# Where the down projection's operands begin: its weight chunks 160 bytes and the gated activations 96 bytes further on

## The chip, the core and the metric

The kernel runs on one core of one Trainium2 chip. The metric is the device time of one execution in microseconds; the kernel before took 497.76 us, the median of three runs between 497.63 and 497.88. Profiles are of one execution each. TensorE is written PE in the profile, its weight loads PEld, VectorE DVE, ScalarE ACT, GpSimd POOL, SyncE SP.

## What is computed

The program is one layer of a decoder trunk on 256 tokens of 1024 channels, in float32:

```python
mix = hybrid_mixer(x, w_in, ...)                 # mLSTM and attention branches, gated, projected
x = layer_norm(ALPHA * x + mix, ln1_g, ln1_b)
u = causal_dwconv(einsum("bsd,df->bsf", x, w_up), conv_ffn)      # 1024 -> 2 x 2816, 3 taps
g, up = split(u, 2)
ffn = einsum("bsf,fd->bsd", silu(g) * up, w_down)                # 2816 -> 1024
x = layer_norm(ALPHA * x + ffn, ln2_g, ln2_b)
```

The change is in the last three lines: `silu(g) * up` is what the text calls the gated activations, `w_down` the down projection.

## The kernel before

**Weights come as a stream of chunks.** `chunk_order` (line 45) lists 81 chunks of 128 x 2048 floats (1 MB) in the order of use: 4 "o", then four groups of 8 (qm, qb, km, kb, vm, vb, ga, gb), 8 for the branch projections (wa, wb), 4 for the output projection (wo), then the MLP: up 0 to 3, then eight times (dn d, up 2d+4, up 2d+5), then up 20, up 21, dn 8, dn 9, dn 10. The main loop of `run` (line 304) takes one chunk per turn. In a turn it issues the element work that the last step left, splits the chunk that is due in two steps, starts the DMA of the chunk five steps ahead on SyncE, and runs `step_<kind>`, which issues the matmuls.

**Every product is three products.** A float32 operand is kept as a high part in float32r (names ending in h) and a rest (l). `split_into` (line 92) makes them: a cast on ScalarE (line 94) and a subtraction on VectorE (line 95). `mm3` (line 125) then issues high x high, high x rest and rest x high, lines 128, 129 and 130, into the same accumulator. In `tensor.matmul(out, stationary, moving)` the second operand is loaded into the array by a LDWEIGHTS of 128 columns, and the third streams past it. So each line of `mm3` has one row of PE and one of PEld in the profile.

**Where an operand begins.** The high and rest parts of a chunk live in tiles of 2176 floats (8704 bytes, 34 x 256), three buffers each (tags "wh" and "wl"). `split_parts` (line 101) puts the chunk at an offset of `shift(kind, i)` floats in its tile:

```python
a = shift(*self.order[s])
wh, wl = wh[:, a:a + KT * 264], wl[:, a:a + KT * 264]
```

`shift` (line 61) is 48 for vm, vb, o; 56 for wa, wb; 8 for up 2; 0 for wo and dn; 16 for the rest. All slices that a matmul takes of an operand lie 512 or 1024 bytes apart (chunk 3 of "o" alone differs), so the start modulo 256 is the same for every matmul of a step. The program's allocation gives these starts (bytes modulo 256):

| step | moving operand | stationary operand | moving columns |
|---|---|---|---|
| o 0, o 1 | weights 64 | x 64 | 512 |
| qm, qb, km, kb, ga, gb | x 64 | weights 128 | 256 |
| vm, vb | weights 0 | x 64 (vm's first: a copy at 128) | 256 |
| wa, wb | y 224 | weights 32 | 256 |
| wo ("mix") | weights 64 | merged 128 | 256 |
| up 0, up 1 | weights 0 | x1 64 | 256 |
| up 2 | x1 64 | weights 96 | 256 |
| up 3 to 21 | x1 64 | weights 128 | 256 |
| dn, before | weights 64 | gated activations 128 | 512 and 256 |
| side work: pss, psl | 128 | 128 | 256 (and 128) |
| side work: pso | 224 | 128 | 256 (and 128) |

up 0 and up 1 have tiles of their own ("ahead").

**The MLP.** `step_up` (line 940) computes one chunk of the up projection, 48 matmuls of 256 moving columns into `ps_up`. `up_evac` (line 987) applies the three convolution taps (lines 999 and 1003, into `cu`), the gate, and splits the result into `hh` and `hl` (tags "hh" and "hlo", 128 x 256 float32r, six buffers each). These come from the pool "ffn", opened at `s == first["up"]` (line 328), and so do `tu`, `cu` and `nmr`. `step_dn` (line 1018) multiplies two such pairs (stationary) by one chunk of `w_down` (moving) into five accumulators called `ffn` that stay open for the whole MLP. For dn 0 to 7 that is 30 matmuls in the order: for each half of the chunk, 6 of 512 columns (tokens 0 to 127), then 3 of 512 and 6 of 256 (tokens 128 to 255). The last three chunks are taken together: 36 of 512 columns for the first tokens, 18 of 512 and then 36 of 256 for the others. In all there are 198 matmuls of 512 columns and 132 of 256. `finish` (line 1082) then normalises and stores the second half of the tokens.

Of the kernel before, what the change touches and what calls it, by code (L numbers as in the profile page):

```python
# [10 lines left out]
F32 = mybir.dt.float32  # L11
# [7 lines left out]
P = 128  # L19
# [41 lines left out]
def shift(kind, i):  # L61

    if (kind, i) == ("up", 2):

        return 8
    if kind in ("vm", "vb", "o"):
        return 48
    if kind in ("wa", "wb"):
        return 56
    return 0 if kind in ("wo", "dn") else 16  # L70


class Kernel:
# [27 lines left out]
    def split_parts(self, s):  # L101
        if s >= len(self.order) or s in self.w:
            return []
        raw = self.raw.pop(s)
        if s in self.extra:
            wh, wl = self.extra.pop(s)
        else:
            wh = self.stream.tile([P, WCOLS], F32R, tag="wh", name=f"wh{s}", bufs=3)
            wl = self.stream.tile([P, WCOLS], F32R, tag="wl", name=f"wl{s}", bufs=3)
            a = shift(*self.order[s])  # L110
            wh, wl = wh[:, a:a + KT * 264], wl[:, a:a + KT * 264]
        if s == 3:

            vh, vl = (t.rearrange("p (k f) -> p k f", k=KT) for t in (wh, wl))
            vr = raw.rearrange("p (k f) -> p k f", k=KT)
            cuts = [tuple(t[:, 4 * i:4 * i + 4, 0:256] for t in (vh, vl, vr)) for i in range(2)]
            cuts.append((vh[:, :, 256:264], vl[:, :, 256:264], self.wif))
        else:
            wh, wl = wh[:, 0:2048], wl[:, 0:2048]
            cuts = [tuple(t[:, i * 1024:(i + 1) * 1024] for t in (wh, wl, raw)) for i in range(2)]  # L120
        self.w[s] = (wh, wl)
        return [lambda c=c: self.split_into(*c) for c in cuts]
# [54 lines left out]
    def run(self):  # L177
# [126 lines left out]
        for s, (kind, i) in enumerate(self.order):  # L304
            if s == 8:
                self.elem_work(s, self.split_parts(s + 2))
                pre_cm.__exit__(None, None, None)
                self.open_att(att_cm.__enter__())
            if s == first["wa"]:
                self.elem_work(s)  # L310
                att_cm.__exit__(None, None, None)
                mix_cm.__exit__(None, None, None)
                self.open_post(post_cm.__enter__())
                mg = mg_cm.__enter__()
                self.mgh = mg.tile([P, KT, S], F32R, name="mgh")
                self.mgl = mg.tile([P, KT, S], F32R, name="mgl")
            if s == first["wo"]:
                self.elem_work(s)
                y_cm.__exit__(None, None, None)
                zp = ahead_cm.__enter__()  # L320
                for j in range(2):
                    self.extra[first["up"] + j] = tuple(
                        zp.tile([P, 2112], F32R, name=f"ahead{n}{j}")[:, 8:8 + 2048] for n in "hl")
            if s == first["up"]:
                self.elem_work(s)
                mg_cm.__exit__(None, None, None)
                self.fp = ffn_cm.__enter__()
            late = s == first["up"]
            self.elem_work(s, [] if late or s == 8 else self.split_parts(s + 2))
            self.load(s + 5)  # L330
            if s in (first["wo"], first["wo"] + 1):
                self.split(s + 4)
            getattr(self, "step_" + kind)(s, i, bo)
            for f in self.side_pe.pop(s, []):
                f()
            if late:
                self.split(s + 2)
# [832 lines left out]
```

## Time and profile before

| what | value |
|---|---|
| median of three runs | 497.76 us (497.63 to 497.88) |
| the profiled execution: its time | 497.07 us |
| its span, first to last instruction | 495.2 us |
| PE busy | 482.3 us, 3889 matmuls |
| DVE, ACT, POOL busy | 369.6, 288.4, 29.5 us |
| the MLP's matmuls, first to last | 298.2 to 486.1 us of the span |

A row of a group of instructions reads: line, engine, operation, output<-inputs, shape, count, busy time and mean duration of one, idle time of the engine just before. A matmul's duration holds its way through the array, so it is longer than the distance from its start to that of the next. This distance is called the **pitch** below. On an engine that never waits, the sum of the pitches is the time. A row of the timeline reads: start in us, duration in us, engine, line, operation, output<-inputs, shape, count.

### The profile page before, as it was taken

To read this page: it belongs to the slowest core of one execution; us is meant where nothing else is said; L and a number is where in the kernel's file an instruction comes from. 1 tells how busy PE (TensorE), PEld (TensorE's weight loads), DVE (VectorE), ACT (ScalarE), POOL (GpSimd) and SP (SyncE) were. 2 spreads that over 40 slices of the span, in tenths; PEclk is the share of its full clock that TensorE was granted. 3 is DMA by queue.
4 is the path that set the end of the run, shared out by engine and by line. 5 is a ranking of instruction groups with operands and counts; after the bars stand their busy time and mean duration, and the time that the engine had idled before them with its cause. 6 is when DMAs were issued, how large, how long until landed. Compare 5 with 4: busy or idle time off the path is not lost.

```text
span 495.2 us, 9470 instructions
## 1 busy us (share of the span) xinstructions
PE 482.3 (97%) x3889; PEld 466.5 (94%) x3889; DVE 369.6 (75%) x662; ACT 288.4 (58%) x478; POOL 29.5 (6%) x46
## 2 busy tenths in 40 slices
PE   7999999999999999999999999999999999999992
PEld 4899999999999999999999999999999999999982
DVE  5776995788588858885777788788667766866886
ACT  5657867495749665866655524666544555554610
POOL 0400011002000110002000001000000000000001
PEclk9999999999999999999999999999999999999997
DMA  7984555555554655444945672745555456444202
GB/s 254 359 300 151 204 191 205 177 179 184 193 173 175 196 180 187 169 171 148 364 171 182 222 276 86 255 148 205 212 203 177 164 185 241 171 171 171 86 1 85
DMA packets 19036, 93.74 MB, mean 189 GB/s; under 512 B 4625, under 2 KB 5913, under 8 KB 9009
## 3 DMA queue, kind: packets, MB, share of 16 engines
q1 hardware_dynamic: 14834, 87.08, 49.5%
q0 software_dynamic: 4160, 6.07, 3.9%
q8 instruction: 30, 0.49, 0.4%
q14 instruction: 12, 0.10, 0.1%
HBM read 92.05 MB, written 2.63 MB: 191 GB/s over the span
## 4 chain that ended last, share of the span: by engine, by line
PE 94%; DMA 2%; DVE 1%; SPq 1%; ACT 0%; issue 0%; POOL 0%; POOLq 0%
PE ps_up L130 8%; PE ps_up L128 8%; PE ps_up L129 8%; PE ffn L130 4%; PE ffn L129 4%; PE ffn L128 4%; PE ps_vm L128 2%; PE ps_qm L128 2%; PE ps_vm L130 2%; PE ps_vm L129 2%; PE ps_vb L130 1%; PE ps_vb L128 1%; PE ps_vb L129 1%; PE mix L128 1%; PE ps_wb L129 1%; PE ps_wa L129 1%
## 5 line engine op out<-in xcount | busy, mean ns | idle before, releaser
L95 DVE TENSOR_TENSOR wl<-raw,wh 128x1024 fp32r<-128x1024 f32 (+1 forms) x162 | 187.8, 1199 | 28.3 <-ACT wh L94 28.0
L94 ACT CAST wh<-raw 128x1024 fp32r<-128x1024 f32 (+1 forms) x162 | 158.8, 1030 | 10.8 <-DMA raw<-in_wst_dram 7.2
L128 PE MATMUL ps_up<-x1h,wh 128*128 128x256 f32 x320 | 90.0, 281 | 0.0
L130 PE MATMUL ps_up<-x1h,wl 128*128 128x256 f32 x320 | 89.9, 281 | 0.0
L129 PE MATMUL ps_up<-x1l,wh 128*128 128x256 f32 x320 | 89.9, 281 | 0.0
L129 PEld LDWEIGHTS ps_up<-x1l,wh 128*128 128x128 f32 x320 | 61.3, 192 | 0.0
L130 PEld LDWEIGHTS ps_up<-x1h,wl 128*128 128x128 f32 x320 | 60.1, 188 | 0.0
L128 PEld LDWEIGHTS ps_up<-x1h,wh 128*128 128x128 f32 x320 | 60.1, 188 | 0.0
L1003 DVE SCALAR_TENSOR_TENSOR cu<-ps_up,vec,cu 128x255 f32<-128x255 f32 (+1 forms) x80 | 33.0, 475 | 27.1 <-ACT cu L999 26.9
L130 PE MATMUL ffn<-wh,hl 128*128 128x512 f32 (+1 forms) x110 | 38.4, 349 | 0.0
L129 PE MATMUL ffn<-wl,hh 128*128 128x512 f32 (+1 forms) x110 | 38.4, 349 | 0.0
L128 PE MATMUL ffn<-wh,hh 128*128 128x512 f32 (+1 forms) x110 | 38.3, 349 | 0.0
L94 ACT CAST hh<-cu 128x256 fp32r<-128x256 f32 x22 | 8.9, 407 | 42.9 <-DVE cu L1011 42.9
L999 ACT ACTIVATE cu<-ps_up,vec 128x256 f32<-128x256 f32 x40 | 16.8, 471 | 28.8 <-PE ps_up L130 28.0
L129 PEld LDWEIGHTS ffn<-wl,hh 128*128 128x128 f32 x110 | 20.8, 189 | 3.0
L128 PEld LDWEIGHTS ffn<-wh,hh 128*128 128x128 f32 x110 | 20.7, 188 | 3.0
L130 PEld LDWEIGHTS ffn<-wh,hl 128*128 128x128 f32 x110 | 20.7, 188 | 2.9
L128 PE MATMUL ps_vb<-wh,xth 128*128 128x256 f32 x64 | 18.1, 283 | 0.0
L128 PE MATMUL ps_gb<-xth,wh 128*128 128x256 f32 x64 | 18.0, 282 | 0.0
L129 PE MATMUL ps_vm<-wl,xth 128*128 128x256 f32 x64 | 17.9, 280 | 0.0
L130 PE MATMUL ps_vm<-wh,xtl 128*128 128x256 f32 x64 | 17.9, 280 | 0.0
L128 PE MATMUL mix<-wh,mgh 128*128 128x256 f32 x64 | 17.8, 279 | 0.0
(292 smaller groups left out, 1424.9 us busy)
## 6 DMA issues: line engine op xcount, KB each, us to landing
raw<-in_wst_dram SPq DMA_DIRECT2D x78, 1024.0 KB, 4.9
raw<-in_wst_dram SPq DMA_DIRECT2D x8, 256.0 KB, 4.7
lnrow<-in_rows_dram POOLq DMA_DIRECT2D x4, 512.0 KB, 6.7
band<-table POOLq DMA_DIRECT2D x4, 384.0 KB, 12.4
xraw<-in_xt_dram SPq DMA_DIRECT2D x8, 128.0 KB, 4.6
raw<-in_wst_dram SPq DMA_DIRECT2D x2, 512.0 KB, 6.8
toe<-band POOLq DMA_DIRECT2D x4, 256.0 KB, 3.5
xtok<-in_x_dram POOLq DMA_DIRECT2D x1, 1024.0 KB, 7.3
```

The source lines that it names most:

```text
L94: self.nc.scalar.copy(wh, raw)
L95: self.nc.vector.tensor_sub(wl, raw, wh.bitcast(F32))
L128: mm(ps, ah if first is None else first, bh, start=start, stop=False)
L129: mm(ps, ah, bl, start=False, stop=False)
L130: mm(ps, al, bh, start=False, stop=stop)
L999: act.activation(cu[:, j, :], ps[:, j, :], AF.Copy, scale=tap(2, j))
L1003: v.scalar_tensor_tensor(cu[:, j, o:], ps[:, j, :S - o], tap(t, j), cu[:, j, o:], op0=ALU.mult, op1=ALU.add)
```

## The change

`shift` returns 40 for "dn" instead of 0, and the pool "ffn" gets a first tile of 24 floats that nothing uses.

```diff
@@ shift
         return 48
     if kind in ("wa", "wb"):
         return 56
-    return 0 if kind in ("wo", "dn") else 16
+    if kind == "dn":
+
+        return 40
+    return 0 if kind == "wo" else 16
@@ run, in the main loop, at s == first["up"]
                 self.elem_work(s)
                 mg_cm.__exit__(None, None, None)
                 self.fp = ffn_cm.__enter__()
+
+                self.fp.tile([P, 24], F32, name="gap")
```

The chunks of dn begin 40 x 4 = 160 bytes further on, at 64 + 160 = 224 modulo 256. The tiles of the pool "ffn" (`tu`, `cu`, `hh`, `hl`, `nmr`) lie 24 x 4 = 96 bytes further on, so `hh` and `hl` begin at 128 + 96 = 224. No instruction is added, removed or moved, and no wait.

## The prediction

> **What bounds the kernel now.** I read the page first: its engine line, the clock, and the chain that ended last.
>
> ```profile
> span 495.2 us, 9470 instructions
> ...
> PE 482.3 (97%) x3889; PEld 466.5 (94%) x3889; DVE 369.6 (75%) x662; ACT 288.4 (58%) x478; POOL 29.5 (6%) x46
> ...
> PEclk9999999999999999999999999999999999999997
> ...
> PE 94%; DMA 2%; DVE 1%; SPq 1%; ACT 0%; issue 0%; POOL 0%; POOLq 0%
> ```
>
> TensorE is busy for 97% of the span, holds 94% of the chain, and its granted clock is full in all slices but the last. Next, the view of waits for PE alone, and the busy times from 350 us on:
>
> ```profile
> PE ps_o L162 <- ACT wh L94: 1.4, 2, 1.0
> PE warm_ps L199 <- DVE warm L196: 1.2, 1, 1.2
> PE ps_o L129 <- DVE wl L95: 1.2, 1, 1.2
> ...
> 350.00:495.00 145.00, 136.10 (x999) 128.66 (x997) 102.23 (x169) 67.73 (x109) 3.04 (x4) 0.98 0.42 152
> ```
>
> That is every wait of PE: 3.8 us, all before 20 us. In the MLP it never waits, so its time there is the sum of the pitches of its matmuls. DVE (102 of 145 us), ACT (68) and the DMA (0.42) have room: with the 4.5 us of the forecast taken from this stretch, DVE is busy for 102 of 140.5 us, 73%. So the only question is how long a matmul takes.
>
> Equal matmuls do not take equal times. From the timeline, the first matmul of a stretch and the first after it:
>
> ```profile
> 12.38 0.39 PE L162 MATMUL ps_o<-wh,xth 128*128 128x512 f32 x1
> ...
> 17.82 0.28 PE L128 MATMUL ps_o<-wh,xth 128*128 128x256 f32 x1
> ...
> 232.00 0.28 PE L128 MATMUL ps_wa<-yah,wh 128*128 128x256 f32 x1
> ...
> 275.53 0.28 PE L128 MATMUL mix<-wh,mgh 128*128 128x256 f32 x1
> ...
> 322.70 0.39 PE L128 MATMUL ffn<-wh,hh 128*128 128x512 f32 x1
> ...
> 328.29 0.28 PE L128 MATMUL ps_up<-x1h,wh 128*128 128x256 f32 x1
> ...
> 339.60 0.39 PE L128 MATMUL ffn<-wh,hh 128*128 128x512 f32 x1
> ...
> 471.90 0.40 PE L128 MATMUL ffn<-wh,hh 128*128 128x512 f32 x1
> ...
> 480.30 0.40 PE L128 MATMUL ffn<-wh,hh 128*128 128x512 f32 x1
> ```
>
> By the code these stretches hold 24, 384, 30, 96 and 36 matmuls. The pitches:
> - 512 columns: 5.44 / 24 = 226.7 ns in "o", 8.40 / 36 = 233.3 ns in ffn, 6.6 ns more;
> - 256 columns: 43.53 / 384 = 113.4 ns in wa and wb, 11.31 / 96 = 117.8 ns in up, 4.4 ns more.
>
> I call the lower pitches quick and the others slow. The mean durations by form say the same of whole groups (the last row is that of "o" between 12.4 and 17.5 us):
>
> ```profile
> L128 PE MATMUL ps_up<-x1h,wh 128*128 128x256 f32 x320 | 90.0, 281 | 0.0
> ...
> L130 PE MATMUL ffn<-wh,hl 128*128 128x512 f32 x66 | 26.1, 395 | 0.0
> ...
> L128 PE MATMUL ffn<-wh,hh 128*128 128x512 f32 x66 | 26.0, 394 | 0.0
> ...
> L128 PE MATMUL ffn<-wh,hh 128*128 128x256 f32 x44 | 12.3, 280 | 0.0
> L130 PE MATMUL ffn<-wh,hl 128*128 128x256 f32 x44 | 12.3, 279 | 0.0
> L129 PE MATMUL ffn<-wl,hh 128*128 128x256 f32 x44 | 12.3, 279 | 0.0
> ...
> L162 PE MATMUL ps_o0b<-wl,xth 128*128 128x512 f32 x4 | 1.6, 389 | 0.0
> ```
>
> The 256-column matmuls of ffn lie between: a quick one lasts 276 and a slow one 281 ns (next fence), so their 279.3 is 3.3 above quick: a pitch of about 116.7.
>
> Start addresses alone do not fix the state. up 0 and up 1 share their operands' starts (moving 0, stationary 64), yet the groups between 298.5 and 302.9 us (first row) and between 306 and 310.2 us differ:
>
> ```profile
> L128 PE MATMUL ps_up<-aheadh,x1h 128*128 128x256 f32 x13 | 3.7, 281 | 0.0
> ...
> L128 PE MATMUL ps_up<-aheadh,x1h 128*128 128x256 f32 x14 | 3.9, 276 | 0.0
> ```
>
> So with the stationary operand 64 bytes ahead of the moving one, 256 columns have two states, each of which lasts until something disturbs it. The 512-column matmuls show two pairs: 64/64 (distance 0) is quick in "o", 64/128 (distance 64) slow in ffn. Since ffn stands between all up steps after up 3, I read the trace so: ffn's pair holds ffn itself slow, and hands each up step the slow state.
>
> **The change part by part.** No instruction comes or goes. The pair of dn goes from 64/128 to 224/224, distance 0. Three terms follow, and a fourth at nothing.
>
> *1. ffn, 512 columns.* 54 of the 198 run in one stretch at the end (36 + 18), 144 in blocks of 9. For distance 0 I have "o": 226.7 once settled, and this on the way there, soon after a wait for the cast:
>
> ```profile
> 7.58 0.40 PE L162 MATMUL ps_o0b<-wh,xth 128*128 128x512 f32 x1
> ...
> 9.66 0.39 PE L162 MATMUL ps_o<-wl,xth 128*128 128x512 f32 x1
> ```
>
> Nine matmuls in 2.08 us: 231 ns. The end stretch settles: 54 x -6.6 = -0.36 us. The blocks of 9 gain between 2.3 (never settled) and 6.6; I take the middle, 4.45, for they do not begin from a wait: 144 x -4.45 = -0.64 us.
>
> *2. ffn, 256 columns.* Distance 0 at 256 columns is shown only by short side work, pss (128/128), whose rows give the least, median and longest duration; pso (224/128) stands for another bad pair:
>
> ```profile
> L129 PE MATMUL pss<-qml,kmh x8: 280/282/287, 60.2 to 210.4; 128*128 128x256 f32 x8
> L130 PE MATMUL pss<-qmh,kml x8: 279/280/285, 60.3 to 210.6; 128*128 128x256 f32 x8
> ...
> L756 PE MATMUL pso<-pth,vbl x8: 282/284/285, 81.6 to 231.9; 128*128 128x256 f32 x8
> ```
>
> pss's medians are 4 and 6 ns above quick; these matmuls come a few at a time after a wait and need not be settled. I take their mean, +5, a pitch of 118.4, as the only rows of distance 0: 132 x (118.4 - 116.7) = +0.22 us. The ends are quick, 132 x -3.3 = -0.44, and pso's +8, a pitch of 121.4: +0.62. Terms 1 and 2 together: -0.78 us, between -1.75 (all 198 settled, 1.31, and 0.44) and +0.6 (nothing at 512 columns, pso's pitch at 256).
>
> *3. up 4 to 21.* 18 x 48 = 864 matmuls, all behind a dn step, at 117.8 now. What decides is the handover: the moving operand will go from 224 to 64, with the stationary one at 128. Before has that same handover from pso to qm; in the fence are pso's last matmul, qm's first and fourth, and the first after qm's 48:
>
> ```profile
> 82.21 0.28 PE L756 MATMUL pso<-pth,vbl 128*128 128x256 f32 x1
> 82.34 0.28 PE L128 MATMUL ps_qm<-xth,wh 128*128 128x256 f32 x1
> ...
> 82.69 0.28 PE L128 MATMUL ps_qm<-xth,wh 128*128 128x256 f32 x1
> ...
> 87.79 0.28 PE L128 MATMUL ps_qb<-xth,wh 128*128 128x256 f32 x1
> ```
>
> Out of a slow pso, qm needs three matmuls (0.35 us) and then runs 45 in 5.10 us: 113.3, quick. wb to mix is the same handover (224 to 64, stationary 128), out of a quick stretch; mix between 276 and 291 us is quick too (first row below). Against these stands kb to vm, where the moving operand goes from 64 to 0: slow from the first matmul, six in 0.71 us, though kb was quick.
>
> ```profile
> L128 PE MATMUL mix<-wh,mgh 128*128 128x256 f32 x45 | 12.4, 276 | 0.0
> ...
> 104.00 0.28 PE L130 MATMUL ps_kb<-xth,wl 128*128 128x256 f32 x1
> 104.11 0.28 PE L128 MATMUL ps_vm<-wh,xfirst 128*128 128x256 f32 x1
> ...
> 104.82 0.28 PE L128 MATMUL ps_vm<-wh,xth 128*128 128x256 f32 x1
> ```
>
> So a handover can go either way, but the one from 224 to 64 went to quick from both states. I take it: 864 x -4.4 = -3.80 us, less some 10 ns of settling at each of the 8 handovers, +0.1: -3.7 us. The other end is 0, since slow is what these steps have already. A loss I exclude: their own pair does not change, and it has shown two states only.
>
> *4. At nothing:* `tu`, `cu` and `nmr` move by 96 bytes as well. They are written and read by ACT and DVE (`tu` by 8 transposes too), which PE does not wait for; with that cover gone, a change in their speed would show as a wait of PE in the MLP, where there is none. up 0 to 3 run ahead of the first dn step and keep their time.
>
> The sum is -0.8 - 3.7 = -4.5 us. Against the profiled execution, 497.07 us (span 495.2 and 1.9 around it), that is 492.6. The median of the three runs lies 0.69 higher, so the forecast is 497.76 - 4.5 = **493.3 us**, and with the ends of terms 1 and 2 alone 492.3 to 494.7.
>
> **The rivals.**
>
> *The up steps stay slow.* Then only terms 1 and 2 are left: 497.0 us, between 496.0 and 498.4. For it speaks that slow lasts as well as quick does (11.31 us without a break), and that kb to vm went to slow. Against it speaks the handover of pso to qm.
>
> *Half of them turn.* Blocks may end in different phases: -0.8 - 1.85 gives 495.1. Against it: the eight blocks are alike in every start address.
>
> *224/224 is a bad pair: slower.* The place is the 330 matmuls of ffn. Moving 224 is quick with stationary 32 (wa, wb), but with 128 it costs pso 8 ns over quick per 256 columns. If 224 has such a cost with 224 too, the 512-column matmuls come to 226.7 + 16 = 242.7, that is 198 x 9.4 = +1.9 us, and those of 256 columns to +0.6, while up stays slow: 497.76 + 2.5 = 500.3 us. It decides from about 2 ns per 256 columns above today's ffn (198 x 2 + 132 = 528 such units make 1.0 us). Against it: distance 0 settled at 226.7 in "o", and pso's distance is another.
>
> *The starts do not matter.* The pitches would then come from something else in these stretches, and the time stays 497.8 us. Against it: the clock is full in both, the shapes and lines are the same, and the up 0 and up 1 groups differ within 8 us of each other. [...]
>
> **How the numbers follow.** Up quick: 0.56. Half: 0.08. Up stays slow: 0.20. Slower: 0.10. No effect: 0.06. The likeliest gives 493.3 us. Its own range with that of the half case, the third's middle and the fifth hold the time in over 8 of 10 cases when I reach from 492.4 to 497.9; the slower rival and the far end of the third are left out. A measurement of this kernel can tell about 0.2%, 1.0 us, from no change. Faster by more than that are the first two cases and a quarter of the third: 0.56 + 0.08 + 0.05 = 0.69. Slower: 0.10. Within 0.2%: the rest of the third and the fifth, 0.15 + 0.06 = 0.21.
>
> **What would show it.** Term 1: the mean duration of ffn's 512-column matmuls falls from about 394 towards 389 ns, and the end stretch of 36 takes 8.16 instead of 8.40 us. Term 2: 256-column ffn rows at 281 rather than 279. Term 3: the rows of ps_up at lines 128 to 130 fall from 281 towards 277 ns, two up steps take 10.9 instead of 11.31 us, and up 2 and 3 alone stay at 281. PE still has no wait after 20 us. The forecast is wrong if up's rows stay at 281, or if ffn's rise above 400 and 282.

## The result, and the profile after

The changed kernel takes 493.81 us (median of 22 runs, 492.47 to 495.46), the kernel before, run beside it on the same chips, 497.36 us (22 runs, 491.88 to 498.92): a ratio of 0.9939, 95% interval 0.9923 to 0.9955. The forecast was 493.3. The profiled execution of after took 492.93 us with a span of 490.9, so the spans differ by 4.3 us, where the sum of the terms was 4.5. The medians differ by 3.55 only, for two reasons. Before's runs are not of one kind: 6 of its 22 lie between 491.9 and 494.8, the others between 496.8 and 499, with a median of 497.5. And the profiled run of after is 0.9 us below after's median. All 22 runs of after lie below 495.5, where before has only its short ones: what the times show is that the long runs are gone, not that the best run got shorter.

The page of after, the lines that answer to those of before (lines of the code stand three to five further down, so `mm3` issues from 131 to 133 now):

```profile
span 490.9 us, 9470 instructions
...
PE 479.7 (98%) x3889; PEld 464.3 (95%) x3889; DVE 369.8 (75%) x662; ACT 287.2 (59%) x478; POOL 31.1 (6%) x46
...
PEclk9999999999999999999999999999999999999997
...
PE 97%; DVE 1%; DMA 1%; ACT 0%; POOL 0%; issue 0%; SPq 0%; POOLq 0%
...
L131 PE MATMUL ps_up<-x1h,wh 128*128 128x256 f32 x320 | 88.6, 277 | 0.0
```

Nothing came or went, the granted clock is the same (a mean of 0.993, before 0.994), and PE holds still more of the chain (97% for 94%). What changed is the mean of the up row: 277 ns for 281, and of these 320 matmuls 32 belong to up 2 and 3, which did not change. The whole view of PE's waits is now

```profile
PE warm_ps L202 <- DVE warm L199: 1.2, 1, 1.2
PE ps_o L165 <- ACT wh L97: 0.9, 1, 0.9
```

so no wait appeared in the MLP: from 20 to 486 us the view is empty. The groups of the MLP by form, 298 to 482 us of after (count, busy us, mean ns):

```profile
L133 PE MATMUL ffn<-wh,hl 128*128 128x512 f32 x66 | 25.8, 392 | 0.0
L131 PE MATMUL ffn<-wh,hh 128*128 128x512 f32 x66 | 25.8, 391 | 0.0
...
L133 PE MATMUL ffn<-wh,hl 128*128 128x256 f32 x44 | 12.4, 282 | 0.0
L131 PE MATMUL ffn<-wh,hh 128*128 128x256 f32 x44 | 12.4, 281 | 0.0
```

ffn's wide matmuls (512 columns) fell by 3 ns only (from 395 and 394), its narrow ones (256) rose by 3 and 1 (from 279 and 280). And the timeline of PE in after: up 6's first matmul, the first after up 6 and 7, the end stretch's first, its 37th and its 55th (the first of 256 columns), and the last matmul.

```profile
344.52 0.28 PE L131 MATMUL ps_up<-x1h,wh 128*128 128x256 f32 x1
...
355.41 0.39 PE L131 MATMUL ffn<-wh,hh 128*128 128x512 f32 x1
...
465.05 0.39 PE L131 MATMUL ffn<-wh,hh 128*128 128x512 f32 x1
...
473.25 0.39 PE L131 MATMUL ffn<-wh,hh 128*128 128x512 f32 x1
...
477.33 0.28 PE L131 MATMUL ffn<-wh,hh 128*128 128x256 f32 x1
...
481.52 0.28 PE L133 MATMUL ffn<-wh,hl 128*128 128x256 f32 x1
```

Two up steps take 10.89 us for 96 matmuls, 113.4 ns each (before 11.31 and 117.8). The first 36 of the end stretch take 8.20 us (before 8.40), the next 18 run at 4.08 / 18 = 226.7 ns, and the narrow ones behind them at 4.19 / 35 = 119.7.

Subtracting each start from the next, over the whole timeline, gives this account of the stretch from dn 0's first matmul to the last matmul:

| part | matmuls | pitch before, ns | pitch after, ns | us |
|---|---|---|---|---|
| up 4 to 21 | 864 | 117.8 | 113.4 | -3.77 |
| ffn, 512 columns, blocks | 144 | 232.7 | 230.4 | -0.33 |
| ffn, 512 columns, end stretch | 54 | 233.2 | 227.4 | -0.31 |
| ffn, 256 columns, blocks | 96 | 116.0 | 118.5 | +0.24 |
| ffn, 256 columns, end stretch | 36 | 117.8 | 119.8 | +0.07 |

That is -4.10 us (163.13 to 159.03). The remaining 0.2 of the 4.3 lies ahead of dn 0, which starts at 322.49 instead of 322.70. I do not count it to the change: in two more profiles of before dn 0 starts at 323.86 and 323.78. Below, "the stretch" is always this one: it is free of what varies ahead of it.

### The profile page after: what moved, and what is told of

It reads as the page before. It is cut to its first block, busy times and chain, and to the rows that moved or that the text cites. A ratio compares the mean times of both kernels' runs of the same rounds, so it can differ in the third digit from the quotient of the medians.

```text
span 490.9 us, 9470 instructions
## 1 busy us (share of the span) xinstructions
PE 479.7 (98%) x3889; PEld 464.3 (95%) x3889; DVE 369.8 (75%) x662; ACT 287.2 (59%) x478; POOL 31.1 (6%) x46
## 4 chain that ended last, share of the span: by engine, by line
PE 97%; DVE 1%; DMA 1%; ACT 0%; POOL 0%; issue 0%; SPq 0%; POOLq 0%
PE ps_up L133 8%; PE ps_up L131 8%; PE ps_up L132 8%; PE ffn L132 4%; PE ffn L133 4%; PE ffn L131 4%; PE ps_vm L131 2%; PE ps_qm L131 2%; PE ps_vm L133 2%; PE ps_vm L132 2%; PE ps_vb L133 1%; PE ps_vb L131 1%; PE ps_vb L132 1%; PE mix L131 1%; PE ps_wb L132 1%; PE ps_wa L132 1%
## 5 line engine op out<-in xcount | busy, mean ns | idle before, releaser
L131 PE MATMUL ps_up<-x1h,wh 128*128 128x256 f32 x320 | 88.6, 277 | 0.0
L133 PE MATMUL ps_up<-x1h,wl 128*128 128x256 f32 x320 | 88.6, 277 | 0.0
L132 PE MATMUL ps_up<-x1l,wh 128*128 128x256 f32 x320 | 88.5, 276 | 0.0
L132 PEld LDWEIGHTS ps_up<-x1l,wh 128*128 128x128 f32 x320 | 60.1, 188 | 0.0
L915 POOL TENSOR_TENSOR rs<-rs,mhalf 128x1 f32<-128x1 f32 x4 | 2.7, 666 | 243.5 <-DVE rs L914 243.5
```

Of the source, the lines that this page charges most:

```text
L131: mm(ps, ah if first is None else first, bh, start=start, stop=False)
L132: mm(ps, ah, bl, start=False, stop=False)
L133: mm(ps, al, bh, start=False, stop=stop)
L915: nc.gpsimd.tensor_tensor(st["rs"], st["rs"], self.mhalf[:, 0:1], op=ALU.pow)
```

## The experiments

The prediction's theory was: at distance 0 the pair of dn runs its 512 columns quick, and the jump of the moving operand from 224 to 64 hands the up steps the quick state. A pair is written as moving/stationary; its distance is the stationary start minus the moving one, modulo 256. Four kernels change the two starts one by one. Before's median beside these four was 497.34 us, but 11 of its 31 runs were short ones, between 492.1 and 494.1, so the ratios below say little, and the traces decide. Each edit is against after.

**1. The weights alone** (dn 224/128, distance 160).

```diff
-                self.fp.tile([P, 24], F32, name="gap")
```

> Weights of dn at 224, activations left at 128 (half of the change). Theory (the handover of the moving start, 224 to 64, turns the up steps quick, the pair sets ffn's own pitch): up 4 to 21 at 113.4 ns as in the changed kernel, -3.8 us; ffn's pair is pso's, so 256 columns at 120 to 122 ns and 512 columns not settled, 231 to 243 ns, which is between +0.1 and +2.6 us; in all 1.2 to 3.7 us below the kernel before. Rival (distance 0 in ffn is what turns the up steps quick): up stays at 117.8 ns and the time is 0 to 2.6 us above before.

497.94 us (10 runs), ratio 1.0006 (0.9972 to 1.0040). ffn is about as expected, 234.1 and 119.0 ns in the blocks, but up stays at 117.8 from the first matmul to the last, its rows at 281 ns (between 298 and 484 us):

```profile
L131 PE MATMUL ps_up<-x1h,wh 128*128 128x256 f32 x320 | 90.0, 281 | 0.0
```

The jump from 224 to 64 is there; it did not suffice in this execution. The 10 runs are of two kinds again, 7 between 497.9 and 499.8 and 3 between 494.4 and 495.4, and only a long one was profiled.

**2. The activations alone** (dn 64/224, distance 160).

```diff
     if kind == "dn":
 
-        return 40
+        return 0
```

> Activations at 224, weights of dn left at 64 (the other half). Theory: the moving start stays 64 over the handover, ffn's pair 64/224 is not distance 0 or 64, so up stays slow at 117.8 ns unless ffn happens to leave it quick; ffn at about 231 and 119 to 120 ns; within 0.5 us of before. Rival (distance 0 does it): the same, up slow. This run tells the halves apart, not the theories.

494.64 us (10 runs), ratio 0.9971 (0.9941 to 1.0001). Up is quick, 113.4, though the moving operand stays at 64 throughout, which neither the theory nor the rival had:

```profile
L131 PE MATMUL ps_up<-x1h,wh 128*128 128x256 f32 x320 | 88.6, 277 | 0.0
```

ffn is at 233.6 and 119.2 in the blocks, about as in 1. So neither the jump nor a quick ffn is needed. The stretch is 159.87 us, 3.26 under before: up gives 3.76, and ffn takes back 0.50.

**3. Distance 0 without a jump** (dn 64/64).

```diff
-        return 40
+        return 0
...
-                self.fp.tile([P, 24], F32, name="gap")
+                self.fp.tile([P, 48], F32, name="gap")
```

> Both operands of dn at 64: distance 0 as in the change, but the moving start does not jump at the handover. Theory (the jump from 224 to 64 turns up quick): ffn as in the changed kernel (512 columns 226.7 ns in the end stretch, 256 columns 120), up stays at 117.8: 0.5 us below before. Rival (distance 0 turns up quick): up at 113.4 and 4 to 4.5 us below before, like the changed kernel.

497.63 us (10 runs), ratio 1.0030 (0.9996 to 1.0064). This is the sharpest comparison with after, for ffn itself runs nearly the same in both (here 229.7 in the blocks and 227.2 in the end stretch at 512 columns, 118.5 and 119.8 at 256; after has 230.4, 227.4, 118.5 and 119.8). The timeline at the handover from the second dn block to up 6, first of after, then of this kernel:

```profile
344.28 0.28 PE L132 MATMUL ffn<-wl,hh 128*128 128x256 f32 x1
344.40 0.28 PE L133 MATMUL ffn<-wh,hl 128*128 128x256 f32 x1
344.52 0.28 PE L131 MATMUL ps_up<-x1h,wh 128*128 128x256 f32 x1
344.63 0.28 PE L132 MATMUL ps_up<-x1l,wh 128*128 128x256 f32 x1
344.74 0.28 PE L133 MATMUL ps_up<-x1h,wl 128*128 128x256 f32 x1
```

```profile
345.91 0.28 PE L132 MATMUL ffn<-wl,hh 128*128 128x256 f32 x1
346.03 0.28 PE L133 MATMUL ffn<-wh,hl 128*128 128x256 f32 x1
346.15 0.28 PE L131 MATMUL ps_up<-x1h,wh 128*128 128x256 f32 x1
346.27 0.28 PE L132 MATMUL ps_up<-x1l,wh 128*128 128x256 f32 x1
346.38 0.28 PE L133 MATMUL ps_up<-x1h,wl 128*128 128x256 f32 x1
```

ffn's last two matmuls keep the same step in both, 0.12 us. From the first up matmul on, the two rows fall apart: 0.22 us for two in after, 0.23 here, and so on without a break, 5.44 us for 48 in after (two steps: 10.89) and 5.65 here. The up steps' own operands have the same starts in both, and the two kernels differ in nothing but dn's shift and the gap, so in these two profiles the state of the up steps, 113.4 or 117.7 ns, went with what ran ahead of them.

**4. Distance 64, elsewhere** (dn 224/32).

```diff
-                self.fp.tile([P, 24], F32, name="gap")
+                self.fp.tile([P, 40], F32, name="gap")
```

> Weights of dn at 224, activations at 32: the pair of wa and wb (distance 64), with the jump from 224 to 64 at the handover. Theory: up 4 to 21 at 113.4 ns (-3.8 us); ffn's 512 columns slow at 233, its 256 columns between 113.4 and 118; 3.6 to 4.4 us below before. Rival (distance 0 in ffn turns up quick): up at 117.8, within 0.5 us of before.

494.82 us (10 runs), ratio 0.9970 (0.9940 to 1.0001). ffn's wide matmuls are slow at 233.0 and 233.4, as at 64/128. Up is quick again, 113.5, after three or four matmuls of settling. And the end stretch's narrow matmuls, 479 to 484 us, are quick at distance 64 (113.7; 119.8 in after):

```profile
L132 PE MATMUL ffn<-wl,hh 128*128 128x256 f32 x12 | 3.3, 276 | 0.0
L133 PE MATMUL ffn<-wh,hl 128*128 128x256 f32 x12 | 3.3, 276 | 0.0
L131 PE MATMUL ffn<-wh,hh 128*128 128x256 f32 x11 | 3.0, 276 | 0.0
```

For distance 0 two rivals stood: any jump of the moving start at the handover turns up quick (A), or it takes the jump from 224 (B). Neither covers experiments 1 and 2, whose distance is 160. Distance 0 at two other places tells them apart; before's median beside these and the next two kernels was 497.55 us.

**5 and 6. Distance 0 at 0 and at 128.** The values that `shift` returns for dn are 48 and 16; the gap is 32 floats in the first, and there is none in the second.

> Both operands of dn at 0, distance 0 as at 224/224 and at 64/64, where ffn's pitches were equal to the nanosecond; so only the handover differs: moving 0 to 64, stationary 0 to 128. Theory A (any jump of the moving start at the handover turns up quick): up 4 to 21 at 113.4, total 3.5 to 4.5 us below before. Theory B (it takes the jump from 224; a jump of 64, as kb to vm has it, leaves slow): up at 117.8, about 0.5 us below before. ffn in both: end stretch 226.7, 256 columns 120 ns.

> Both operands of dn at 128, distance 0; at the handover the moving start goes from 128 to 64 and the stationary one stays at 128. Theory A (any jump of the moving start turns up quick): up at 113.4, 3.5 to 4.5 us below before. Theory B (a jump of 64 leaves slow): up at 117.8, about 0.5 us below before. ffn in both: end stretch 226.7, 256 columns 120 ns.

494.66 and 492.88 us, one run each; most of what parts them lies ahead of dn 0, which starts at 324.32 and 322.76. The stretch is 158.96 and 158.89 us, both some 0.1 under after. Up 4 to 21 run at 113.5 in both, at 0/0 and 128/128 as at 224/224. So at distance 0 the place 224 is nothing special for up: three of the four places tried give 113.4 to 113.5, and 64 gives 117.7. In the run of 0/0 up 3 was quick too (all rows of 320.6 to 322.3 us at 276 ns, 281 in after), though nothing ahead of it differs; this was not explained. In these two profiles an up step ran at 276 and at 281 ns with all starts ahead of it the same.

**7. up 2 and 3.** These run ahead of dn and stayed slow in after. The edit takes up 2's own line out of `shift`, so it gets 16 like the other up steps and stands at distance 64 as well.

```diff
-    if (kind, i) == ("up", 2):
-
-        return 8
```

> The changed kernel with up 2 at shift 16 instead of 8, so that its pair is 64/128 (distance 64) like that of the other up steps. Theory (at distance 64 256 columns hold whichever state they were handed, at distance 32 they hold none and hand on slow): up 2 at 113.4 or 117.8 ns instead of 118.3, and after the transposes up 2's second half and up 3 settle quick as mix does after its transposes; 0.1 to 0.45 us less than the changed kernel in up 2 and up 3. Rival (up 3 is slow for another reason, such as the element work of these steps): up 3 stays at 117.8 and the time is that of the changed kernel.

494.06 us (10 runs), ratio 0.9941 (0.9917 to 0.9965), no different from after. Distance 64 did not make up 2 or 3 quick: up 2's mean pitch is 119.6 against 119.9 in after, and up 3's rows, in the same window as above, stay at 281 ns.

```profile
L130 PE MATMUL ps_up<-x1h,wl 128*128 128x256 f32 x6 | 1.7, 281 | 0.0
L128 PE MATMUL ps_up<-x1h,wh 128*128 128x256 f32 x5 | 1.4, 281 | 0.0
L129 PE MATMUL ps_up<-x1l,wh 128*128 128x256 f32 x5 | 1.4, 281 | 0.0
```

The theory missed here: at distance 64 up 3 was quick in the run of 0/0 (276 ns), but in this run it stayed slow (281).

**8. Blocks of one width.** The blocks gained 0.33 - 0.24 = 0.09 us net; by terms 1 and 2 it should have been 0.64 - 96 x 1.7 ns = 0.48. If the cause is that they change between 512 and 256 columns and settle anew each time, blocks of 512 columns alone should gain. The accumulators of the third and fourth quarter share a tile of 512 columns for this:

```diff
-            a1 = [self.ps_side([P, 512], "ffn10"), self.ps_side([P, 256], "ffn11"), self.ps_side([P, 256], "ffn12")]
+            a1 = [self.ps_side([P, 512], "ffn10"), self.ps_side([P, 512], "ffn11")]
...
-                    for ps, cols in self.acc[t]:
+                    for ps, cols in self.wide[t]:
```

> The changed kernel with all of dn 0 to 7 in 512 columns (the accumulators for columns 512 to 767 and 768 to 1023 of the later tokens share a bank; the last three chunks still use 256 columns there). Theory (distance 0 is quick at 512 columns and slow, 120 ns, at 256, and the switches between the two widths unsettle both): a block of dn takes 24 x 226.7 = 5.44 instead of 5.57 us, 8 blocks 1.0 us less than the changed kernel, if the handover to up still goes to quick; up at 113.4. Rival (the state that ffn's last matmuls leave decides, not the jump of the starts): a settled ffn hands up another state, up goes to 117.8 and the kernel is 2.8 us slower than the changed one.

493.61 us (10 runs), ratio 0.9935 (0.9902 to 0.9967), not to be told from after. Its stretch is 158.39 us, 0.64 under after and not the 1.0 expected: the eight blocks take 43.92 us instead of 44.56, at 228.8 per matmul and not 226.7. Up stays at 113.4, so the rival fell. The gain is given back behind the stretch. DVE between 481 and 484 us, in after and in this kernel:

```profile
L907 DVE SCALAR_TENSOR_TENSOR r<-x,ffn 128x256 f32<-128x256 f32 x1 | 0.4, 421 | 0.5 <-PE ffn L133 0.5
```

```profile
L907 DVE SCALAR_TENSOR_TENSOR r<-x,ffn 128x256 f32<-128x256 f32 x2 | 0.8, 412 | 1.3 <-PE ffn L133 1.3
```

With one tile for both, the residual addition of the third quarter, and its statistics (0.43 us), wait for the very last matmul (an idle time of 1.3 us ahead of the addition, ended by PE), where after has them done and idles 0.5 us; from the last matmul to the end of the span it takes 0.8 us longer. (dn 0 also began 0.66 us later in this run, at 323.15, so its span is 491.7.) Separate tiles at the end with wide blocks was not tried.

**9. The pairs by themselves.** 1,780 matmuls on zeros are issued ahead of the unchanged rest of after, 1,768 of them in float32r, without a pause between those of a group; 48 of 256 columns or 36 of 512 for each pair, then 12 handovers to 64/128. Between groups stands one small copy on VectorE. Otherwise the other engines do nothing there but for one broadcast on GpSimd at 16.6 us, and the DMA is all but still from 18 us on (busy share 0.00 in the 3 us from 26, from 32, from 38 and from 67 us, 0.03 in those from 79). The kernel's first loads land before that, during the first group, 64/64 at 256 columns.

```diff
...
+            def go(m, s, n, count):
+                for i in range(count):
+                    a = 2048 + i % 4 * 256 + s // 4
+                    b = i % 3 * 512 + m // 4
+                    mm(ps[:, 0:n], t[:, a:a + P], t[:, b:b + n], start=True, stop=True)
...
```

> The changed kernel with a stretch of 1,780 test matmuls ahead of its work, on zeros, with no DMA into the tiles they read and VectorE and ScalarE still but for a small copy between the groups: groups of 48 of 256 and 36 of 512 columns for each distance of the starts, then 24 at one pair followed by 36 at 64/128. Theory (the two start addresses of one matmul stream set the pitch): distance 0 gives 226.7 ns at 512 and 120 at 256 columns, distance 64 gives 233.3 at 512 and, after a wait, 113.4 at 256 columns, the others lie between 116 and 122 (256) and at 231 to 236 (512); the same at 0, 64 and 224. Handed over to 64/128: from 64/64 and 224/128 slow (117.8), from 0/0, 128/128, 224/224, 224/32 and 64/224 quick (113.4). Rival (the pitches come from other engines or transfers at the same addresses): 113.4 and 226.7 for every pair. The profile also covers the kernel behind it, whose up steps should be as in the changed kernel.

The timeline puts matmuls of one line together, so the pitch is (duration - one) / (count - 1). First groups of 256 columns, settled: 64/64, 64/128, and 224/32; then of 512 columns 64/64 and 64/128:

```profile
13.70 3.16 PE L200 MATMUL probe_ps<-probe_t 128*128 128x256 f32 x25
...
26.63 3.34 PE L200 MATMUL probe_ps<-probe_t 128*128 128x256 f32 x27
...
68.68 3.34 PE L200 MATMUL probe_ps<-probe_t 128*128 128x256 f32 x28
...
85.98 6.05 PE L200 MATMUL probe_ps<-probe_t 128*128 128x512 f32 x26
...
102.83 6.00 PE L200 MATMUL probe_ps<-probe_t 128*128 128x512 f32 x25
```

(3.16 - 0.28) / 24 = 120.0, (3.34 - 0.28) / 26 = 117.7 and 3.06 / 27 = 113.3; then (6.05 - 0.39) / 25 = 226.4 at distance 0, and (6.00 - 0.40) / 24 = 233.3 at distance 64. The mean pitches at the end of each group (its last 16), in ns, moving operand at 64:

| distance | 0 | 32 | 64 | 96 | 128 | 160 | 192 | 224 |
|---|---|---|---|---|---|---|---|---|
| 256 columns | 120.0 | 118.4 | 117.8 | 117.3 | 118.7 | 120.1 | 117.8 | 117.8 |
| 512 columns | 226.7 | 233.3 | 233.3 | 234.7 | 232.9 | 233.2 | 228.9 | 233.3 |

With the moving operand at 0 or 224, distance 0 gives the same, 120.0 and 226.7; distance 64 gives 113.4 and 233.3. So for the distances tried at more than one place, 0 and 64, groups of one distance have one pitch (120.0 and 226.7; 233.3), but for one case: 256 columns at distance 64 are quick (113.4) or slow (117.8). The expectation had 64/128 quick after a wait; it was slow (117.8). The rival that other engines' traffic makes the pitch is out: with that traffic gone (a DMA share of 0.00 between 26 and 29 us and between 67 and 70, the granted clock 1.00 in both) the pairs still differ, 117.7 and 113.3, and 224/224 and 0/0, which run when the loads have landed, repeat the 120.0 of 64/64. The kernel behind the test has after's stretch, 159.03 us.

The handovers, 24 matmuls at a pair and then 36 at 64/128, whose settled pitch follows in ns:

| from (moving/stationary) | 64/128 runs at |
|---|---|
| 0/0, 32/32, 96/96, 128/128, 160/160, 192/192, 224/224 | 113.3 to 113.4 |
| 64/64 | 117.8 |
| 224/32, 224/128, 64/224 | 113.3 to 113.4 |
| 0/64 | 117.8 |

The rows of the second part from 32/32, 64/64 and 224/224:

```profile
196.51 3.34 PE L200 MATMUL probe_ps<-probe_t 128*128 128x256 f32 x28
...
203.84 3.34 PE L200 MATMUL probe_ps<-probe_t 128*128 128x256 f32 x27
...
240.56 3.34 PE L200 MATMUL probe_ps<-probe_t 128*128 128x256 f32 x28
```

In the same 3.34 us pass 28 matmuls, or 27. Out of distance 0 only the pair that shares the moving start 64 fails to turn, as in experiment 3. In these groups the state was not simply passed on: distance 0 runs at 120.0 itself and hands on quick, and 0/64 runs quick itself (113.3) and hands on slow. One row differs from the expectation and from the kernel: 224/128 turned here and did not in experiment 1.

**10 and 11. The kernel before, two more profiles,** to catch one of its short runs.

> The kernel before once more, since its runs lie between 491.9 and 499.9 us in groups some 4 us apart. Theory (up 4 to 21 keep whichever state they were handed): a run near 497.5 has up at 117.8 throughout, a run near 493.5 has it at 113.4. Rival: the groups differ elsewhere (start of the first loads, clock).

> The kernel before a third time, to see a second one of the groups its runs fall into: up 4 to 21 at 117.8 ns in a run near 497.5 us, at 113.4 ns in a run near 493.5 us (theory: they keep the state they were handed), or another difference than that (rival).

498.21 and 498.23 us, up at 117.8 throughout both times. What differs in its short runs was not seen, so that they have up quick stays a guess.

**12. The starts of experiment 1 with another way of leaving off.** If starts alone decide, 224/128 must always hand on slow in this kernel. The edits of 1 and 8 together leave all starts as in 1, but the six matmuls ahead of an up step have 512 columns.

> The weights alone at 224 (activations at 128: the starts of the first experiment), with dn 0 to 7 all in 512 columns as in the wide-block run. One look. Theory (at a handover to moving 64, stationary 128 the outcome hangs on the starts and on the point of the cycle at which ffn leaves off): the last matmuls ahead of each up step are now six of 512 columns rather than six of 256, so the outcome can change; if it does, up 4 to 21 fall from 117.8 to 113.4 ns, their rows from 281 to 277, and the time is about 497.9 - 3.8 - 0.6 = 493.5 us. I give this one half. Rival (the starts of the two pairs alone decide): up stays at 117.8 and 281, and the time is 497.9 less at most 0.6 for the blocks, 497.3 us. ffn's 512-column matmuls stay near 233 in both.

494.98 us, one run beside 497.41 of before. The timeline of the second handover, of experiment 1 and of this kernel:

```profile
345.25 0.29 PE L132 MATMUL ffn<-wl,hh 128*128 128x256 f32 x1
345.38 0.28 PE L133 MATMUL ffn<-wh,hl 128*128 128x256 f32 x1
345.50 0.28 PE L131 MATMUL ps_up<-x1h,wh 128*128 128x256 f32 x1
345.61 0.28 PE L132 MATMUL ps_up<-x1l,wh 128*128 128x256 f32 x1
345.73 0.28 PE L133 MATMUL ps_up<-x1h,wl 128*128 128x256 f32 x1
345.85 0.28 PE L131 MATMUL ps_up<-x1h,wh 128*128 128x256 f32 x1
```

```profile
345.00 0.39 PE L132 MATMUL ffn<-wl,hh 128*128 128x512 f32 x1
345.23 0.39 PE L133 MATMUL ffn<-wh,hl 128*128 128x512 f32 x1
345.46 0.28 PE L131 MATMUL ps_up<-x1h,wh 128*128 128x256 f32 x1
345.58 0.28 PE L132 MATMUL ps_up<-x1l,wh 128*128 128x256 f32 x1
345.69 0.28 PE L133 MATMUL ps_up<-x1h,wl 128*128 128x256 f32 x1
345.81 0.28 PE L131 MATMUL ps_up<-x1h,wh 128*128 128x256 f32 x1
```

Up settles within three matmuls here (five at the first handover) and runs at 113.4 in all 18 steps, 97.99 us against 101.75 in experiment 1, while ffn's wide matmuls stay slow, 233.4. The same pair of starts before, the same after, and two outcomes, 117.8 and 113.4: in these two profiles the starts alone did not decide. That the width of the last six matmuls did it is not shown by one execution of each kernel, since experiment 1's own runs are of two kinds. The stretch is 159.60 us (163.69 in experiment 1). The time is 1.5 over the expectation: some 0.8 is the shared tile's late addition of experiment 8, which I had left out, dn 0 began 0.45 us later than in 1, and the blocks gained 0.33 rather than 0.6.

## Why the prediction was right, and where it was off

**What bounds the kernel.** Right: PE had no wait in the MLP and has none now (the last ended before 20 us in both profiles), and the time went with the pitches: -4.10 us of pitches in a span shorter by 4.3.

**Term 3, the up steps, -3.7.** Measured -3.77. That the state lasts, and that it goes with what runs ahead of an up step, is shown by after and experiment 3 side by side (113.4 and 117.7 over whole up steps) and by the bare handovers (113.3 and 117.8). It need not be the state that ffn has itself: in after its 256 columns run at 118.5 and up turns quick. The 0.1 for settling at the handover was not needed: the pitches of up are quick from its first matmul on. The step behind it, "the one from 224 to 64 went to quick from both states", was luck in part. The rows to hand came from 224/128 (pso to qm) and 224/32 (wb to mix), none from distance 0, and they were compared by the moving start alone. Experiment 1 has the very pair of pso and stays slow; experiment 2 has no jump of the moving start and turns. For 224/224 those rows gave the right answer; as a rule they were too few. The rival "the up steps stay slow" was no idle one: of the seven pairs tried for dn in this kernel, 64/64 shows it, and 224/128 in one profile of two.

**Term 1, 512 columns, -0.36 and -0.64.** The end stretch, -0.31, settled as "o" did. The blocks gave -0.33, half of the forecast: 2.3 ns per matmul, the lower end ("never settled"). The middle was taken because blocks "do not begin from a wait"; my reading, an estimate, is that the settling begins again at each change of width and pair. Experiment 8 speaks for it: without the change of width the blocks run at 228.8, not at 230.4.

**Term 2, 256 columns, +0.22.** Measured +0.31. In the blocks 118.5 stood against the 118.4 taken; the settled pitch of distance 0 is 120.0 (experiment 9), which the end stretch shows.

**Term 4, at nothing:** no wait appeared.

**The rivals.** "224/224 is a bad pair" fell with 226.7 ns at 512 columns in experiment 9. "The starts do not matter" fell with experiments 3 (117.7 in up, 113.4 in after) and 9 (113.4 to 120.1 at 256 columns). "Half of them turn" did not occur: in each of the profiles either all up steps behind a dn block turned or none.

**Left open:** why the pitch differs with the distance, which no run shows; why 224/128 hands on slow in experiment 1, quick in 9 and 12; and what sets the two kinds of runs that before and experiment 1 have. Up 3's quick pitch in the run of 0/0 suggests one way, for before's pair 64/128 at 256 columns has both states; no short run of before was profiled.

## What to carry to other kernels

When PE never waits, compare the pitch of equal matmuls between stages: 4% between rows of one shape at one clock was 3.77 of the 4.10 us gained here. Two addresses were moved for it; one of them alone, that of the activations, brought 3.26. Here the pitch of the up steps went with the stage ahead (113.4 ns in after, 117.7 in experiment 3, their own starts the same), so a change of starts is judged by the steps behind it as well as by its own. Blocks that change their width ran at 230.4 ns per 512 columns and blocks of one width at 228.8, so widths are worth comparing too; and a saving in the middle must not lengthen what follows the last matmul, as the 0.8 us of experiment 8 did.

## What the runs showed of the hardware

- Float32r matmuls with a weight load each, on zeros, at a mean granted clock of 0.996 (experiment 9): with the moving operand at 64, the groups at eight distances of the two operands' starts modulo 256 settled at 226.7 to 234.7 ns at 512 columns and at 117.3 to 120.1 at 256, where distance 64 at other starts gave 113.4. Distance 0 gave the least of the eight at 512 columns (226.7) and was among the two slowest at 256 columns (120.0). No run shows the cause, and none moves an operand by 256 bytes, so whether 256 is the right modulus was not shown.
- At 256 columns and distance 64 the traces show two pitches, 113.4 and 117.8. Each lasted as long as the stream did: up to 192 matmuls in the kernel (113.3 in after, 117.8 in before), and to the end of a group of 48 with the other engines still (experiment 9: 113.4 and 117.8). After a pause, distance 64 went either way there: 64/128 to slow (117.8), 224/32 and 0/64 to quick (113.4).
